# Opening stage: v of two head pairs made token-major, the last K blocks of each half accumulator by accumulator, one accumulator parked in SBUF

## The chip, the cores and the metric

The kernel runs on one core of a Trainium2 chip. The core has a matrix engine (PE, which multiplies a stationary 128x128 block with a moving block of up to 512 columns and writes to PSUM), a vector engine (DVE), a scalar engine (ACT), a general engine (POOL), and an engine whose queue issues DMAs (SP). SBUF is the working memory of 128 partitions; PSUM has eight banks of 512 float32 per partition. The metric is the time on the device in microseconds, of one launch; less is better.

## What is computed

One layer of a streaming encoder for 1024 tokens of width 1024. What bears on the change is its beginning:

```python
mod = (c_act @ w_ada[l] + b_ada[l])[:, None, :]
sh_m, sc_m, g_m, sh_f, sc_f, g_f = jnp.split(mod, 6, axis=-1)
h = rmsnorm(x, norm_mix_w[l]) * (1 + sc_m) + sh_m
z, xbc, dt_raw, q, k, v = jnp.split(h @ w_in[l], IN_SPLITS, axis=-1)
y_ssd = ssd_mixer(z, xbc, dt_raw, ...)
y_att = chunk_attention(q, k, v, rel_bias[l])
x = x + g_m * (jnp.concatenate([y_ssd, y_att], axis=-1) @ w_out[l])
...
```

The attention has 8 heads of 64 features, which the kernel handles as four pairs of 128 features. A query block of 64 tokens sees its own and the 8 blocks before it, with a bias by relative position. The rest (the mixer, the output projection, a gated feed-forward network with a causal convolution, the final norm) comes after it and isn't touched.

## The kernel before

**Numbers in two parts.** Products are made exact enough by splitting each float32 operand into a high and a low part of the type fp32r. `mm3` (lines 75 to 78) issues three matmuls for each product: high by high, high by low, low by high. `split` (lines 80 to 86) makes the two parts, the high one as a copy on ACT (line 85) and the low one as a difference on DVE (line 86); with a scale, these are lines 82 and 83.

**The opening stage** (lines 272 to 304) makes q, k and v of pairs 0 and 1. Tokens are handled in two halves of 512 (`hh`), the contraction over 1024 features in eight K blocks of 128 (`kt`). For a K block of half 0 it loads two columns of `w_ada` and reduces them on DVE (`mod_col`, line 134) to the scale `amix` and the shift `bmix`, loads the block's weights `w_first[kt]` and splits them into `wsh` and `wsl` or `wsl2` (read through `ws_lo`). Then, in both halves, four transposes on PE (line 290) turn the normalised token tiles `xts` into a PSUM tile `tps`; `h_block` (lines 241 to 244) applies scale and shift on ACT into `hf`, of which there is one buffer, and DVE writes the high and low parts hH and hL; and six accumulators in six PSUM banks (tag `acc0`) each get one `mm3` of 512 columns: q0, k0, v0, q1, k1, v1, with features in the partitions and tokens in the columns. Of the other two banks (tag `tp0`) the transposes use one each.

**Evacuation.** After the last K block of a half, `evac_qkv` (lines 217 to 236) is called for the six accumulators. q: two scaled splits of 64 partitions. k: two splits, and four DMAs that copy kh and kl to the other 64 partitions (line 228, issued by SP). v: a copy to SBUF on ACT (line 230), four transposes on PE (line 232), and a split into the tile `v`, which has tokens in its partitions, as the weighted sum of the attention needs it.

**Memory that is used again.** The q and k tiles and the eight tiles `xts` share twelve buffers (`qkp`): pair 1's kh and kl lie where token tiles 4 to 7 were, which half 1 still transposes. So k1 of half 0 can't be evacuated before half 1's transposes are done. When the opening stage ends, its pool `s0` (weights, `hf`, and so on) and its banks `ps0` are given back, and the attention's tiles (`pp` for softmax rows, `bp` for bias, `ptp`, and the PSUM pool `ps1` with the tags s, tp, acc and pv) take their place.

**The attention** (`attention`, line 403, with `attn_scores` and `attn_pv`) goes through four steps `u` of two token tiles each for a pair. Scores on PE (line 335), bias and row maximum on DVE (line 347), exponential on ACT (line 350), reciprocal on DVE (line 352), scaling on POOL (line 353), transposes on PE (lines 379, 382), the weighted sum on PE (lines 390, 391). Between scores and sums of some steps, functions given as `extra` are traced: for pairs 1 and 2 these are the GEMMs of q, k and v of the next pair (`gemm_part`, line 431; 512-column matmuls named acc<-hH,wh and so on in the profile). They still use the v path with transposes.

**Order.** A planner places the instructions of all engines by a simulated timeline, so the order on an engine isn't that of the program text: in the profile part of pair 2's GEMM already runs during pair 0's attention. Where `T.on` is set, `InOrder` (lines 45 to 61) chains each PE instruction behind the one traced before it. SP issues its DMAs in order, and one that waits holds back those behind it.

Of the kernel before, what the change touches and what calls it, by code (L numbers as in the profile page):

```python
# [10 lines left out]
F32 = mybir.dt.float32  # L11
# [5 lines left out]
P = 128  # L17
# [47 lines left out]
def tile_block(ctx: ExitStack, tc: tile.TileContext, x, crep, pk, w_ada, w_first, w_ft, w_z,  # L65
# [111 lines left out]
    qkp = es_at.enter_context(tc.tile_pool(name="qkp", bufs=12, side="right"))  # L177
    vp = es_at.enter_context(tc.tile_pool(name="vp", bufs=2, side="right"))
    es_0 = ExitStack()
# [31 lines left out]
    qk = {}  # L211

    def new_pair(p):
        qk[p] = {n: [qk_tile(F32R) for _ in range(2)] for n in ("q", "kh", "kl")}
        qk[p]["v"] = vp.tile([P, NT, 2, 2, 64], F32R, tag="v", name="v")

# [52 lines left out]
    for st in range(4):  # L269
        norm1(st)  # L270
    adw = wu.tile([P, 2, 1024], F32, tag="w2", bufs=1, name="adat2")
    for hh in range(2):
        accs = [ps0.tile([P, 512], F32, tag="acc0", bufs=6, name="acc0") for _ in range(6)]
        for kt in range(KT):
            if hh == 0:
# [7 lines left out]
                for st in range(4, NT):  # L283
                    if XL[st - 4] == kt:
                        V.tensor_copy(xts[st][:, 0:1], amix[:, kt:kt + 1])
                        nc.sync.dma_start(xts[st], x[st * P:(st + 1) * P, :])
                        norm1(st)
            tps = ps0.tile([P, 512], F32, tag="tp0", bufs=2, name="tp0")
            for j in range(4):
                T.transpose(tps[:, j * P:(j + 1) * P], xts[4 * hh + j][:, kt * P:(kt + 1) * P], ident)  # L290
            tmp = s0.tile([P, 512], F32, tag="hf", bufs=1, name="hf")
            hi, lo = ht(hh, kt)
            h_block(tps, amix, bmix, kt, hi, lo, tmp)
            for t in range(6):
                w = slice(t * P, (t + 1) * P)
                mm3(c4(accs[t]), wsh[:, kt, w], ws_lo(kt)[:, w], hi, lo,
                    kt == 0, kt == KT - 1)
        for t in range(6):
            tmp = tps = None
            if t % 3 == 2:  # L300
                tmp = s0.tile([P, 512], F32, tag="hf", bufs=1, name="hfv")
                tps = ps0.tile([P, 512], F32, tag="tp0", bufs=2, name="tpv")
            evac_qkv(t // 3, t % 3, hh, accs[t], tmp, tps)
    es_0.close()
# [4 lines left out]
    ptp = es_at.enter_context(tc.tile_pool(name="ptp", bufs=1, side="right", reuse_waits="tile"))  # L309
    es_p1 = ExitStack()  # L310
    ps1 = es_p1.enter_context(tc.tile_pool(name="ps1", bufs=1, space=PSUM, reuse_waits="tile"))
# [45 lines left out]
    def attn_pv(p, u, h, p0, p1):  # L357
# [7 lines left out]
        if lo0 < lo1:  # L365
            blocks.append((lo0, 0, 128))
        pv = ps1.tile([P, 512], F32, tag="pv", bufs=1, name="pv")[:, 0:256]
        nb = len(blocks)
# [62 lines left out]
    def gemm_part(p, which):  # L431
        if which == 0:
            new_pair(p)
        wh, wl = wu_pair(w_ft[8 + 3 * (p - 2) + which], A, G)
        outs = [ps1.tile([P, 512], F32, tag="acc", bufs=1, name="acc") for _ in range(2)]
        gemm_ft(wh, wl, outs)
        for hh in range(2):
            tmp = tps = None
            if which == 2:
                tmp, tps = p_tile()[:, 0:512], tp_tile()  # L440
            evac_qkv(p, which, hh, outs[hh], tmp, tps)
# [17 lines left out]
    part = lambda p, w: (lambda: gemm_part(p, w))  # L459
    attention(0)  # L460
    for p in (1, 2):
# [113 lines left out]
    def z_tile(ch, st, wz):  # L575
        if st % 4 < 2:
            ps = ps1.tile([P, 512], F32, tag=("acc", "pv")[st % 4], bufs=1, name="zps")[:, 0:260]
        else:
# [816 lines left out]
def _layout(i):  # L1395
# [12 lines left out]
    pairs = [w[:, p * P:(p + 1) * P] for p in range(4) for w in (wq, wk, wv)]  # L1408
    w_first = np.concatenate(pairs[0:6], axis=1).reshape(KT, P, 768)
    ft = [w_in[:, 512 + P * j:512 + P * (j + 1)] for j in range(8)] + pairs[6:]  # L1410
# [31 lines left out]
```

## Time and profile before

| what | value |
|---|---|
| median of 3 runs (lowest, highest) | 1228.65 us (1228.55, 1231.7) |
| the profiled execution: its time | 1230.44 us |
| the profiled execution: its span | 1228.7 us |
| mean granted PE clock | 0.984 |
| DMA, mean over the span | 123 GB/s |

The busy time of each engine in the stretches around the opening stage, from the view that sums it by stretches:

| stretch, us | what | PE busy | DVE busy | ACT busy | POOL busy | granted clock |
|---|---|---|---|---|---|---|
| 18 to 57 | half 0 | 38.21 | 36.63 | 18.19 | 9.37 | 1.00 |
| 57 to 64 | between the halves | 3.88 | 5.76 | 5.22 | 1.48 | 0.77 |
| 64 to 101 | half 1 | 36.52 | 11.01 | 9.30 | 0.00 | 0.95 |
| 101 to 106 | before the attention | 1.99 | 4.82 | 3.97 | 0.00 | 0.91 |
| 106 to 128 | attention, pair 0 | 20.88 | 13.64 | 13.46 | 14.73 | 0.87 |

How to read the profile lines that follow. A line of the timeline gives the start and the length in us, the engine, the line of the kernel, the operation, the tile written and the tiles read, the shape and the count of merged instructions; in brackets stands how long the engine stood idle before it, and what it waited for. PE is the matmul, PEld the load of the stationary operand, SPq the issue of a DMA. Matmuls are pipelined, so a line's length is longer than the distance to the next start; the distance is what a matmul costs in a stream. A line grouped by operation gives the count, the total busy time in us, the mean in ns, and the idle time ahead of the group with what ended it.

### The profile page before, as it was taken

Reading aid. Unit: us, or ns where it says so; the run is one execution under the profiler, and the core shown is the slowest. Engines: PE = TensorE matmul, PEld = TensorE weight load, DVE = VectorE, ACT = ScalarE, POOL = GpSimd, SP = SyncE. Lnnn points to the kernel's source line nnn. Section 1 sums busy time; section 2 is a strip of 40 time slices with the busy share of each in tenths; the row PEclk is TensorE's granted clock in tenths of the full one; section 3 lists DMA queues with packets and bytes.
Section 4 is the critical chain, followed back from the end, with each engine's and each line's share of the span. In section 5 each row is a group of like instructions: output and inputs, shape, how many; then the busy total and the mean of one; then the engine's idle time right before and its main releaser. Section 6 shows DMA issues by size and latency. Waiting matters only on the chain.

```text
span 1228.7 us, 15497 instructions
## 1 busy us (share of the span) xinstructions
PE 1169.9 (95%) x5722; PEld 978.2 (80%) x5722; DVE 945.2 (77%) x1419; ACT 590.0 (48%) x994; POOL 198.9 (16%) x174
## 2 busy tenths in 40 slices
PE   5898999989999989999899999999999999999995
PEld 3787788878878968888688888888888888888884
DVE  7835655589699678747799988988889869766976
ACT  4525656573333567666554433443334445433443
POOL 1303655474220034300000000000000000000002
PEclk9998999999999989999999999999999999999998
DMA  9712112134356301132122233222232277733533
GB/s 335 266 37 67 48 44 65 46 114 169 107 179 212 121 1 53 37 127 95 54 84 106 100 129 129 78 93 106 111 129 78 95 282 271 275 121 121 172 120 137
DMA packets 56395, 150.86 MB, mean 123 GB/s; under 512 B 5632, under 2 KB 5760, under 8 KB 54912
## 3 DMA queue, kind: packets, MB, share of 16 engines
q1 hardware_dynamic: 49264, 125.49, 29.9%
q10 hardware_dynamic: 7056, 24.38, 5.0%
q8 instruction: 45, 0.74, 0.2%
q14 instruction: 30, 0.25, 0.1%
HBM read 116.56 MB, written 29.10 MB: 119 GB/s over the span
## 4 chain that ended last, share of the span: by engine, by line
PE 68%; DVE 6%; ACT 1%; DMA 1%; issue 1%; POOL 0%; DVEq 0%; POOLq 0%; SPq 0%; ACTq 0%
PE wops L629 6%; PE dn L76 6%; PE dn L77 6%; PE dn L78 6%; PE uY L76 5%; PE uY L77 5%; PE uY L78 5%; PE uZ L76 3%; PE uZ L77 3%; PE uZ L78 3%; PE uX L77 3%; PE uX L76 3%; PE uX L78 3%; PE s L76 2%; PE s L77 2%; PE s L78 2%
## 5 line engine op out<-in xcount | busy, mean ns | idle before, releaser
L861 POOL TENSOR_TENSOR st<-st,mhalf 128x1 f32<-128x1 f32 x16 | 12.7, 799 | 691.8 <-DVE st L860 680.4
L76 PE MATMUL dn<-w 128*128 128x512 f32 x308 | 111.9, 389 | 0.0
L77 PE MATMUL dn<-w 128*128 128x512 f32 x308 | 111.9, 389 | 0.0
L78 PE MATMUL dn<-w 128*128 128x512 f32 x308 | 103.3, 389 | 0.0
L353 POOL TENSOR_SCALAR p<-p,st 128x640 f32<-128x640 f32 (+4 forms) x64 | 98.5, 1554 | 29.1 <-DVE st L352 27.2
L76 PE MATMUL uY<-tH,w 128*128 128x512 f32 x256 | 99.7, 389 | 1.8 <-ACT w L58 1.8
L77 PE MATMUL uY<-tL,w 128*128 128x512 f32 x256 | 99.6, 389 | 0.0
L78 PE MATMUL uY<-tH,w 128*128 128x512 f32 x256 | 99.6, 389 | 0.0
L629 PE MATMUL wops<-hH,yhl 128*128 128x512 f32 x224 | 76.3, 409 | 4.9 <-DVE yhl L86 2.1
L85 ACT ACTIVATE w<-ya 128x1024 fp32r<-128x1024 f32 (+1 forms) x41 | 39.1, 954 | 84.7 <-PE uY L78 82.7
L77 PEld LDWEIGHTS dn<-w 128*128 128x128 f32 x308 | 57.8, 188 | 12.1
L78 PEld LDWEIGHTS dn<-w 128*128 128x128 f32 x308 | 57.8, 188 | 12.0
L76 PEld LDWEIGHTS dn<-w 128*128 128x128 f32 x308 | 57.8, 188 | 11.9
L347 DVE CUSTOM_DVE_ANT_0 p<-s,bias 128x640 f32<-128x640 f32 (+4 forms) x64 | 40.7, 650 | 25.5 <-PE tp L379 8.7
L76 PEld LDWEIGHTS uY<-tH,w 128*128 128x128 f32 x256 | 48.0, 188 | 12.2 <-ACT w L58 2.2
L78 PEld LDWEIGHTS uY<-tH,w 128*128 128x128 f32 x256 | 48.0, 188 | 10.0
L77 PEld LDWEIGHTS uY<-tL,w 128*128 128x128 f32 x256 | 48.1, 188 | 9.9
L86 DVE TENSOR_TENSOR pt<-tp,pt 128x512 fp32r<-128x512 f32 (+2 forms) x72 | 41.8, 595 | 17.4 <-ACT pt L85 10.2
L85 ACT ACTIVATE pt<-tp 128x512 fp32r<-128x512 f32 (+2 forms) x72 | 36.4, 523 | 38.5 <-PE tp L379 17.9
L629 PEld LDWEIGHTS wops<-hH,yhl 128*128 128x128 f32 x224 | 43.1, 194 | 14.7 <-DVE yhl L86 2.5
L85 ACT ACTIVATE w<-xs 128x1024 fp32r<-128x1024 f32 (+1 forms) x41 | 38.9, 952 | 32.2 <-PE uY L78 32.2
L76 PE MATMUL s<-hH,wh 128*128 128x512 f32 x128 | 50.6, 395 | 1.0 <-DVE ct L450 1.0
(432 smaller groups left out, 3405.5 us busy)
## 6 DMA issues: line engine op xcount, KB each, us to landing
gz<-a ACTq DMA_DIRECT2D x10, 1024.0 KB, 5.3
wos<-in_w_ada_dram SPq DMA_DIRECT2D x18, 512.0 KB, 4.4
ya<-in_w_up_dram SPq DMA_DIRECT2D x11, 768.0 KB, 4.0
xs<-in_w_up_dram SPq DMA_DIRECT2D x11, 768.0 KB, 4.1
adat<-in_w_ada_dram SPq DMA_DIRECT2D x16, 512.0 KB, 5.6
raws<-in_w_ft_dram SPq DMA_DIRECT2D x14, 512.0 KB, 3.8
qk<-in_w_ada_dram SPq DMA_DIRECT2D x14, 512.0 KB, 4.4
gy<-a ACTq DMA_DIRECT2D x10, 512.0 KB, 2.6
```

The source lines that it names most:

```text
L76: T.matmul(ps, lh, rh, start=start, stop=False, skip_group_check=more)
L77: T.matmul(ps, lh, rl, start=False, stop=False, skip_group_check=more)
L78: T.matmul(ps, ll, rh, start=False, stop=stop, skip_group_check=more)
L85: i = A.activation(hi, src, AF.Copy) if ehi is A else ehi.tensor_copy(hi, src)
L86: return i, elo.tensor_tensor(lo, src, f32(hi), ALU.subtract)
L347: V.tensor_tensor_reduce(out=dst, in0=src, in1=bsl, scale=-1.0, scalar=3e38, op0=ALU.add, op1=ALU.min, accum_out=nm)
L353: G.tensor_scalar(pv_, pv_, rr, None, op0=ALU.mult)
L629: i = op(*a, **k)
L861: G.tensor_tensor(r, ms, mhalf[:, 0:1], ALU.pow)
```

## The change

The first six column blocks of the weights are put in a new order: q0, k0, q1, k1, v0, v1. v of both pairs is then computed with the token block of h as the stationary operand and the 256 columns of v0 and v1 as the moving one (`first_v`), so that tokens come out in the partitions. Its PSUM tiles `vps` hold two token blocks by 256 columns each and use the tags acc and pv of a pool `psv`, which the attention goes on to use. `evac_v` splits from PSUM straight into one tile `vv` for all pairs (pair p uses part p % 2).

Only four accumulators remain (`acc0` and `acc1`, two banks each). Up to `split_at` (K block 6 in half 0, K block 4 in half 1) the K blocks run one after the other as before. The remaining ones run accumulator by accumulator, with PE's order chained: in half 0 first v, then q0, k0, q1, k1, each evacuated when it is done, except k1, which ACT copies to `k1` in SBUF; in half 1 q0, k0, q1, k1, each evacuated, then the parked `k1`. The remaining K blocks of v of half 1 and their evacuation are traced within step 0 of pair 0's attention. `hf` gets a second buffer.

```diff
@@ -175,7 +175,9 @@
     yp = es_y.enter_context(tc.tile_pool(name="yp", bufs=1, side="right"))
     es_at = ExitStack()
     qkp = es_at.enter_context(tc.tile_pool(name="qkp", bufs=12, side="right"))
-    vp = es_at.enter_context(tc.tile_pool(name="vp", bufs=2, side="right"))
+    vp = es_at.enter_context(tc.tile_pool(name="vp", bufs=1, side="right"))
+    es_p1 = ExitStack()
+    psv = es_p1.enter_context(tc.tile_pool(name="psv", bufs=1, space=PSUM, reuse_waits="tile"))
     es_0 = ExitStack()
     s0 = es_0.enter_context(tc.tile_pool(name="s0", bufs=1, side="right"))
     ps0 = es_0.enter_context(tc.tile_pool(name="ps0", bufs=1, space=PSUM))
@@ -210,9 +212,11 @@
 
     qk = {}
 
+    vv = vp.tile([P, NT, 2, 2, 2, 64], F32R, name="v")
+
     def new_pair(p):
         qk[p] = {n: [qk_tile(F32R) for _ in range(2)] for n in ("q", "kh", "kl")}
-        qk[p]["v"] = vp.tile([P, NT, 2, 2, 64], F32R, tag="v", name="v")
+        qk[p]["v"] = vv[:, :, p % 2]
 
     def evac_qkv(p, which, hh, ps, tmp, tps):
         d = qk[p]
@@ -269,8 +273,37 @@
     for st in range(4):
         norm1(st)
     adw = wu.tile([P, 2, 1024], F32, tag="w2", bufs=1, name="adat2")
+
+    def first_qk(acc, n, hh, kts):
+        w = slice(n * P, (n + 1) * P)
+        for kt in kts:
+            mm3(c4(acc), wsh[:, kt, w], ws_lo(kt)[:, w], *ht(hh, kt), kt == 0, kt == KT - 1)
+
+    def first_v(vps, hh, kts):
+
+        for b, ps in enumerate(vps):
+            for kt in kts:
+                h = T.on
+                T.on, T.last = True, T.last if h else None
+                for j in range(2):
+                    mm3(ps[:, j], hth[hh][:, 2 * b + j, kt, :], htl[hh][:, 2 * b + j, kt, :],
+                        wsh[:, kt, 512:768], ws_lo(kt)[:, 512:768], kt == 0 and j == 0, kt == KT - 1, True)
+                T.on = h
+
+    def evac_v(vps, hh):
+        for b, ps in enumerate(vps):
+            st = 4 * hh + 2 * b
+            o = vv[:, st:st + 2].rearrange("p j q h s d -> p (j q h) s d")
+            split(o[:, :, 0, :], o[:, :, 1, :], ps.rearrange("p j (a d) -> p (j a) d", d=64), A, V)
+
     for hh in range(2):
-        accs = [ps0.tile([P, 512], F32, tag="acc0", bufs=6, name="acc0") for _ in range(6)]
+        accs = [ps0.tile([P, 512], F32, tag="acc0", bufs=2, name="acc0") for _ in range(2)]
+        if hh == 0:
+            tp_ = [ps0.tile([P, 512], F32, tag="tp0", bufs=2, name="tp0")]
+        accs += [ps0.tile([P, 512], F32, tag="acc1", bufs=2, name="acc1") for _ in range(2)]
+        vps = [psv.tile([P, 2, 256], F32, tag=t, bufs=1, name="vps") for t in ("acc", "pv")]
+        split_at = KT - (2, 4)[hh]
+        tail = range(split_at, KT)
         for kt in range(KT):
             if hh == 0:
                 mod_col(SC_M + kt, wu.tile([P, 1024], F32, tag="wh", name="adat"))
@@ -285,29 +318,38 @@
                         V.tensor_copy(xts[st][:, 0:1], amix[:, kt:kt + 1])
                         nc.sync.dma_start(xts[st], x[st * P:(st + 1) * P, :])
                         norm1(st)
-            tps = ps0.tile([P, 512], F32, tag="tp0", bufs=2, name="tp0")
+            tps = tp_.pop() if tp_ else ps0.tile([P, 512], F32, tag="tp0", bufs=2, name="tp0")
             for j in range(4):
                 T.transpose(tps[:, j * P:(j + 1) * P], xts[4 * hh + j][:, kt * P:(kt + 1) * P], ident)
-            tmp = s0.tile([P, 512], F32, tag="hf", bufs=1, name="hf")
+            tmp = s0.tile([P, 512], F32, tag="hf", bufs=2, name="hf")
             hi, lo = ht(hh, kt)
             h_block(tps, amix, bmix, kt, hi, lo, tmp)
-            for t in range(6):
-                w = slice(t * P, (t + 1) * P)
-                mm3(c4(accs[t]), wsh[:, kt, w], ws_lo(kt)[:, w], hi, lo,
-                    kt == 0, kt == KT - 1)
-        for t in range(6):
-            tmp = tps = None
-            if t % 3 == 2:
-                tmp = s0.tile([P, 512], F32, tag="hf", bufs=1, name="hfv")
-                tps = ps0.tile([P, 512], F32, tag="tp0", bufs=2, name="tpv")
-            evac_qkv(t // 3, t % 3, hh, accs[t], tmp, tps)
+            if kt < split_at:
+                for n in range(4):
+                    first_qk(accs[n], n, hh, (kt,))
+                first_v(vps, hh, (kt,))
+        T.on, T.last = True, None
+        if hh == 0:
+            first_v(vps, 0, tail)
+            evac_v(vps, 0)
+            for n in range(4):
+                first_qk(accs[n], n, 0, tail)
+                if n < 3:
+                    evac_qkv(n // 2, n % 2, 0, accs[n], None, None)
+            k1 = s0.tile([P, 512], F32, name="k1")
+            A.activation(k1, accs[3], AF.Copy)
+        else:
+            for n in range(4):
+                first_qk(accs[n], n, 1, tail)
+                evac_qkv(n // 2, n % 2, 1, accs[n], None, None)
+            evac_qkv(1, 1, 0, k1, None, None)
+        T.on = False
     es_0.close()
 
 
     pp = es_at.enter_context(tc.tile_pool(name="pp", bufs=8, side="right", reuse_waits="tile"))
     bp = es_at.enter_context(tc.tile_pool(name="bp", bufs=3, side="right", reuse_waits="tile"))
     ptp = es_at.enter_context(tc.tile_pool(name="ptp", bufs=1, side="right", reuse_waits="tile"))
-    es_p1 = ExitStack()
     ps1 = es_p1.enter_context(tc.tile_pool(name="ps1", bufs=1, space=PSUM, reuse_waits="tile"))
     ya = yp.tile([P, NT, 512], F32, tag="y", name="ya")
     pt = ptp.tile([P, 6, 512], F32R, name="pt")
@@ -364,7 +406,7 @@
         blocks.append((i1, 128, 128))
         if lo0 < lo1:
             blocks.append((lo0, 0, 128))
-        pv = ps1.tile([P, 512], F32, tag="pv", bufs=1, name="pv")[:, 0:256]
+        pv = psv.tile([P, 512], F32, tag="pv", bufs=1, name="pv")[:, 0:256]
         nb = len(blocks)
         done = 0
         while done < nb:
@@ -432,7 +474,7 @@
         if which == 0:
             new_pair(p)
         wh, wl = wu_pair(w_ft[8 + 3 * (p - 2) + which], A, G)
-        outs = [ps1.tile([P, 512], F32, tag="acc", bufs=1, name="acc") for _ in range(2)]
+        outs = [psv.tile([P, 512], F32, tag="acc", bufs=1, name="acc") for _ in range(2)]
         gemm_ft(wh, wl, outs)
         for hh in range(2):
             tmp = tps = None
@@ -457,7 +499,7 @@
         return last.ins
 
     part = lambda p, w: (lambda: gemm_part(p, w))
-    attention(0)
+    attention(0, {0: (lambda: first_v(vps, 1, tail), lambda: evac_v(vps, 1))})
     for p in (1, 2):
         attention(p, {u: [part(p + 1, w) for w in ws] for u, ws in GP.items()})
         for w in GPL:
@@ -574,7 +616,7 @@
 
     def z_tile(ch, st, wz):
         if st % 4 < 2:
-            ps = ps1.tile([P, 512], F32, tag=("acc", "pv")[st % 4], bufs=1, name="zps")[:, 0:260]
+            ps = psv.tile([P, 512], F32, tag=("acc", "pv")[st % 4], bufs=1, name="zps")[:, 0:260]
         else:
             ps = s_tile()[:, 0:260]
         for kt in range(KT):
@@ -1406,7 +1448,7 @@
         axis=1)
     wq, wk, wv = (w_in[:, 1544 + 512 * j:1544 + 512 * (j + 1)] for j in range(3))
     pairs = [w[:, p * P:(p + 1) * P] for p in range(4) for w in (wq, wk, wv)]
-    w_first = np.concatenate(pairs[0:6], axis=1).reshape(KT, P, 768)
+    w_first = np.concatenate([pairs[j] for j in (0, 1, 3, 4, 2, 5)], axis=1).reshape(KT, P, 768)
     ft = [w_in[:, 512 + P * j:512 + P * (j + 1)] for j in range(8)] + pairs[6:]
     w_ft = np.stack([w.reshape(KT, P, P).transpose(1, 0, 2).reshape(P, KT * P) for w in ft])
     wz = np.concatenate([w_in[:, 0:512], w_in[:, 1536:1544]], axis=1)
```

## The prediction, made before the changed kernel was run

> **What bounds the kernel now.** I read the page's first part, the chain of waits, then PE's timeline through the opening stage, then the busy time by stretches.
>
> ```profile
> PE 1169.9 (95%) x5722; PEld 978.2 (80%) x5722; DVE 945.2 (77%) x1419; ACT 590.0 (48%) x994; POOL 198.9 (16%) x174
> PE 68%; DVE 6%; ACT 1%; DMA 1%; issue 1%; POOL 0%; DVEq 0%; POOLq 0%; SPq 0%; ACTq 0%
> ```
>
> PE is the engine that is full and the one the last chain runs through. So what counts is where PE is not multiplying at full rate. In the opening stage that happens at two seams: after the last K block of half 0, and after the last K block of half 1.
>
> ```profile
> 56.53 0.40 PE L78 MATMUL acc<-hH,wsl 128*128 128x512 f32 x1
> 56.77 0.60 PE L232 MATMUL tpv<-ident,hfv 128*128 128x128 f32 x4
> 59.23 0.66 PE L232 MATMUL tpv<-ident,hfv 128*128 128x128 f32 x4 [1.86 <-ACT hfv L230]
> 59.72 0.62 PE L290 MATMUL tp<-ident,qk 128*128 128x128 f32 x4
> 61.61 1.97 PE L290 MATMUL tp<-ident,qk 128*128 128x128 f32 x8 [1.26 <-ACT hf L242]
> 63.23 2.48 PE L76 MATMUL acc<-hH,wsh 128*128 128x512 f32 x5
> 65.51 0.63 PE L77 MATMUL acc<-hL,wsh 128*128 128x512 f32 x1
> 67.22 0.56 PE L77 MATMUL acc<-hL,wsh 128*128 128x512 f32 x1
> ...
> 99.75 0.39 PE L76 MATMUL acc<-hH,wsh 128*128 128x512 f32 x1
> 100.89 0.40 PE L78 MATMUL acc<-hH,wsl 128*128 128x512 f32 x1
> 101.12 0.60 PE L232 MATMUL tpv<-ident,hfv 128*128 128x128 f32 x4
> 103.40 0.66 PE L232 MATMUL tpv<-ident,hfv 128*128 128x128 f32 x4 [1.68 <-ACT hfv L230]
> 103.81 0.42 PE L335 MATMUL s<-qk 128*128 128x128 f32 x2
> 105.56 0.66 PE L335 MATMUL s<-qk 128*128 128x128 f32 x2 [1.33 <-issue]
> 106.02 0.73 PE L76 MATMUL acc<-hH,wh 128*128 128x512 f32 x1
> 111.67 0.52 PE L77 MATMUL acc<-hL,wh 128*128 128x512 f32 x1
> ```
>
> The unit first. From 99.75 to 100.89 lie five starts: 1.14 / 5 = 0.228 us for one 512-column matmul at full rate. From 65.51 to 67.22 lie four: 0.43 us, about half rate.
>
> Seam 1: the last accumulation ends at 56.53 + 0.23 = 56.76 and the next begins at 63.23, 6.47 us later. Inside are 8 transposes of v (L232) and 12 of x (L290); the 12 are needed anyway, at about 0.11 us each 1.3 us. Lost: 5.15 us. Then, from 63.23 to 67.22, nine starts take 3.99 us instead of 2.05: another 1.94.
>
> Seam 2: 101.12 to 106.02 is 4.90 us, of it four 128-column score matmuls (0.24 us) are needed. Lost: 4.66. From 106.02 to 111.67 thirteen starts take 5.65 us instead of 2.96: 2.69. Both seams together lose 14.4 us.
>
> **The change part by part.** *v token-major.* It removes 16 transposes (inside the seams, counted there), the four copies on ACT ahead of them, and PE's waits on those copies. 96 matmuls of 512 columns become 192 of 256. The trace has nearly this shape in the z stage, with new weights for every matmul (the copy's row stands first):
>
> ```profile
> L230 ACT ACTIVATE hfv<-acc 128x512 f32<-128x512 f32 x4 | 2.4, 592 | 0.3 <-PE acc L78 0.2
> ...
> 399.36 0.28 PE L76 MATMUL zps<-wzh,hH 128*128 128x260 f32 x1
> 400.92 0.28 PE L77 MATMUL zps<-wzl,hH 128*128 128x260 f32 x1
> L77 PEld LDWEIGHTS zps<-wzl,hH x64: 187/188/193, 380.5 to 425.8; 128*128 128x128 f32 x64
> ```
>
> Thirteen starts in 1.56 us: 0.120 us at 260 columns, so 0.118 at 256. 192 x 0.118 - 96 x 0.228 = 22.7 - 21.9 = +0.8 us. A load is listed with 188 ns, yet the pitch is 0.120, so loads overlap each other here.
>
> *The end of half 0.* The six first K blocks run as now. Then comes a PE order written by hand: v of blocks 6 and 7, then q0, k0, q1, k1, each with its own two blocks. The second group of v already needs block 7, which now comes last.
>
> ```profile
> 48.60 1.52 PE L76 MATMUL acc<-hH,wsh 128*128 128x512 f32 x6
> 49.40 0.95 DVE L86 TENSOR_TENSOR wsl<-raws,wsh 128x768 fp32r<-128x768 f32 x1
> 50.72 0.69 DVE L244 TENSOR_TENSOR hL<-hf,hH 128x512 fp32r<-128x512 f32 x1
> 53.37 2.88 DVE L267 TENSOR_SCALAR qk<-qk,st 128x1024 f32<-128x1024 f32 x1 [0.75 <-POOL st L117]
> L83 DVE SCALAR_TENSOR_TENSOR qk<-acc,qk 64x512 fp32r<-64x512 f32 x12 | 8.3, 689 | 9.1 <-ACT qk L82 8.8
> ```
>
> hL of block 7 is ready at 50.72 + 0.69 = 51.41; PE, which reaches block 6 at 48.60, will stand before it for about 1 us. Queued behind in the hand-written order are q0 to k1, which nothing may pass. The second hf buffer could bring hL forward at most to where wsl is ready (50.35), a gain of 1; DVE is in order and full there, so I take 0. From 51.41 remain 16 v matmuls (1.9 us) and 24 of 512 columns (5.5 us): half 0 ends at 58.8, 2.0 later than now. In exchange v, q0 and k0 are evacuated meanwhile (each two steps on ACT and two on DVE, about 0.59 and 0.69 us by the rows of L230 and L83). The first h block of half 1 needs the last normalised x tile (53.37 + 2.88 = 56.25), then transposes, ACT and DVE, with some four evacuation steps ahead of it on DVE: about 60. So half 1 starts multiplying at about 60.4, bounds 58.8 (everything hidden) and 63.2 (as now). I take the half rate there as gone, since this gap is a third of the shorter one that it followed. Parking k1 adds one ACT copy of about 0.59 us, hidden in the same stretch; its four evacuation steps and four k copies stay late, since its targets are the buffers of x tiles 4 to 7, which half 1 still transposes.
>
> *Half 1.* 96 x 0.228 + 96 x 0.118 = 33.2 us, plus 24 transposes not yet done, 2.6: the matmuls end at 96.2. The last 5.7 us of these (48 of 256 columns) are v's tail, now traced inside the first attention step. q0, k0, q1, k1 and the parked k1 are evacuated under the tail. The v tail holds banks "acc" and "pv"; acc's part is evacuated (0.59 + 0.69 us) under pv's 24 matmuls. So the GEMM of pair 2 can begin at about 96.5 at full rate, against 106.02 + 2.69: PE is 12.2 us ahead.
>
> *The wait it adds.* The bias tiles and the softmax tiles lie where s0 lay, and v's tail still reads s0's weights. So the bias load can't be issued before v's tail ends; SP issues it in order behind the k copies.
>
> ```profile
> 105.66 0.47 SPq L228 DMA_DIRECT2D qk<-qk  x1
> 105.03 0.54 SPq L408 DMA_DIRECT2D bias<-in_bias_dram  x1
> 108.69 0.14 POOL L409 MEMSET bias<- 64x64 f32 x1 [50.21 <-DMA bias<-in_bias_dram]
> 108.86 0.29 DVE L347 CUSTOM_DVE_ANT_0 p<-s,bias 128x128 f32<-128x128 f32 x1 [2.68 <-POOL bias L409]
> 113.84 0.42 DVE L347 CUSTOM_DVE_ANT_0 p<-s,bias 128x256 f32<-128x256 f32 x1 [1.15 <-PE s L335]
> 115.25 18.66 POOL L353 TENSOR_SCALAR p<-p,st 128x256 f32<-128x256 f32 x12 [1.75 <-DVE st L352]
> 126.60 0.69 DVE L83 SCALAR_TENSOR_TENSOR qk<-acc,qk 64x512 fp32r<-64x512 f32 x1
> ```
>
> Issue to first softmax step: 108.86 - 105.03 = 3.83 us. With the issue between 96.5 and 98.1 (the last k copies ahead of it, about 0.5 us each) I take 97.0; softmax starts at 100.8, 8.0 us earlier. Does PE's 12.2 count, or this 8.0? The first attention pair is paced by POOL, back to back from 115.25 for 18.66 us, and the GEMM of pair 2 stops after its first half until 126.60, when the q tiles it writes become free. So the lower end is nearer. The 1.15 us wait for a score matmul that ran behind half-rate ones should mostly go: I take 8.5.
>
> *After that* the same instructions follow. The busy time by stretches (first column after the length is PE):
>
> ```profile
> 130.00:290.00 160.00, 151.76 (x883) 129.04 (x884) 99.71 (x266) 90.68 (x211) 98.10 (x69) 0.99 0.24 79
> 290.00:330.00 40.00, 40.00 (x216) 34.36 (x215) 29.56 (x40) 15.72 (x26) 8.28 (x5) 1.00 0.26 85
> ```
>
> PE is 95% busy, then wholly, so the shift should be carried to the end. **Sum:** on the profiled execution 1228.7 - 8.5 = 1220.2 us of span (1230.44 as its own time); the median shown is 1228.65, equal to the span, so 1220.2.
>
> **A rule on the half rate.** "TensorE: Matmul & The Clock Gate" of the Trainium skill (part 1) says that the array falls to half rate after an idle window of some 3.4 us and recovers after a busy one of that length; part 4 adds that transposes don't count as busy in the same way. The trace agrees: gaps of 6.5 and 4.9 us, each with little but transposes, were followed by 4.0 and 5.7 us at 0.43 us pitch. By this rule a seam of 1.6 us stays at full rate, as in the sum; but it gives a rival, below.
>
> **The rivals.** (1) *Half rate comes back in the first attention pair.* PE's 24 GEMM matmuls are used up 5.5 us after 96.5, at 102, while scores and transposes come in numbers only from about 105 (113.84 less 8.5). Price: one stretch like the second, 2.7 us; or seam 1 opens until 63.2: 2.8. Together with the forecast that is 1222.9 or 1223.0; with the half rate of seam 1 besides (1.9), 1224.9. For it: the 18.66 us of POOL; against: POOL then hides part of it.
>
> (2) *PE's whole lead counts*: 12.2 us, 1216.5. Against: the POOL row.
>
> (3) *Given back later.* The order of all engines in the attention stage is planned anew. PE lacks 8.2 us of the 160 from 130 to 290; an order with twice these holes gives 1228.4. Nothing in the rows asks for it; nothing excludes it.
>
> (4) *Slower: one v tile for all pairs.* If writing v of pair 2 (or 3) counts as touching the tile that pair 1 (or 2) reads, every later weighted sum of that pair waits for a whole v GEMM, 48 x 0.228 = 10.9 us, at two places: up to 21.9, 1242. It decides from 4.3 us at each. Against it:
>
> ```profile
> 22.74 0.42 DVE L243 CAST hH<-hf 128x512 fp32r<-128x512 f32 x1
> 24.89 0.39 PE L78 MATMUL acc<-hH,wsl 128*128 128x512 f32 x1
> 187.54 0.69 DVE L86 TENSOR_TENSOR v<-tp,v 128x512 fp32r<-128x512 f32 x1 [0.46 <-ACT v L85]
> 192.51 0.33 PE L390 MATMUL pv<-pt,v 128*128 128x256 f32 x1
> ```
>
> DVE writes block 1 of hH at 22.74 while PE reads block 0, interleaved in one tile, until 24.89; and v of pair 2 is complete at 188.2, ahead of the sums from 192.51 on, so at most those before it could be held up.
>
> **How the numbers follow.** Forecast (gain 6.5 to 11): 0.55. Rival 1 (gain 3.7 to 6.5): 0.14. Rival 2: 0.08. Rival 3: 0.15. Rival 4: 0.08. A measurement of this kernel tells about 0.3% (3.7 us) from no change: faster 0.76, same 0.15, slower 0.09. The range 1213.5 to 1228.5 takes in both bounds of the sum (6.9 to 12.2, and the 14.4 of both seams) and half of rival 3.
>
> **What would show it.** In the changed profile: no L232-like transposes before the first attention step; 256-column matmuls at 0.118 us; half 0 ending near 58.8 after a short wait on hL; half 1 starting near 60.4 without 0.43 us pitches; matmuls of half 1 done near 96; first softmax step near 100.8; then the same distance of about 8.5 us up to the end. Wrong would be a first softmax step after 105, a new hole in the attention pairs, or sums of pair 1 or 2 waiting for a v evacuation.

## The result, and the profile after

| | before | after |
|---|---|---|
| median (lowest, highest), 5 runs each | 1228.85 us (1228.55, 1231.7) | 1234.94 us (1233.96, 1236.51) |
| the profiled execution: time, span | 1230.44 us, 1228.7 us | 1236.51 us, 1234.8 us |

The changed kernel is slower by 6.1 us: the ratio is 1.0052, with a 95% interval from 1.0037 to 1.0066. The prediction said 1220.2 us with a range from 1213.5 to 1228.5, so sign and range were both wrong.

First the busy times from the page of the changed kernel:

```profile
PE 1169.8 (95%) x5802; PEld 983.1 (80%) x5802; DVE 944.7 (77%) x1419; ACT 589.0 (48%) x991; POOL 199.9 (16%) x174
```

PE's busy time is that of before to 0.1 us (1169.9 there). So the 6.1 us are not work. They are time in which PE stood still, and the question is where. Following the same events through both traces tells it (us from the start of each span; the columns on the right are experiments of the next section):

| event | predicted | before | after | e1 | e4 | e11 |
|---|---|---|---|---|---|---|
| half 1 starts multiplying | 60.4 | 63.23 | 63.41 | 62.93 | 60.39 | 60.74 |
| GEMM of pair 2 starts | 96.5 | 106.02 | 102.12 | 101.31 | 97.48 | 97.83 |
| first bias load issued | 97.0 | 105.03 | 105.49 | 104.69 | 100.86 | 97.39 |
| first softmax step | 100.8 | 108.86 | 109.72 | 109.25 | 105.26 | 103.87 |
| GEMM of pair 2 goes on | | 130.69 | 129.32 | 128.62 | 124.53 | 123.03 |
| last weighted sum taken over | | 328.5 | 328.6 | 326.4 | 322.2 | 321.8 |
| first state-space matmul (ydp) | | 433.1 | 440.2 | 431.5 | 427.4 | 426.3 |
| span | | 1228.7 | 1234.8 | 1226.9 | 1222.7 | 1222.1 |

Two separate things are in the third and fourth columns. Up to the last sum of the attention at 328.5 the change has gained nothing: the opening stage did not bring what was forecast. And between 328 and 440, in a part that the diff touches only in the pool of two tiles, 7 us are lost. The loss is the whole result, so it comes first.

**The loss at 433 to 440.** The busy time by stretches has it (length, then PE, PEld, DVE, ACT, POOL, granted clock, share of the DMA engines, GB/s). Before:

```profile
400.00:450.00 50.00, 47.56 (x345) 44.55 (x344) 35.16 (x67) 30.59 (x75) 9.25 (x8) 0.97 0.22 75
```

After:

```profile
400.00:450.00 50.00, 43.52 (x314) 41.57 (x313) 34.00 (x65) 27.55 (x67) 8.57 (x8) 0.90 0.23 75
```

PE is busy 4.0 us less, and the clock is lower. PE's timeline there, before:

```profile
432.97 0.28 PE L78 MATMUL s<-wzh,hL 128*128 128x260 f32 x1
433.09 1.89 PE L629 MATMUL ydp<-xdt,th 128*128 128x64 f32 x16
...
437.41 0.71 PE L629 MATMUL xps<-ct,bt 128*128 128x128 f32 x4 [1.05 <-DVE zs L587]
...
439.74 0.79 PE L629 MATMUL wops<-hH,yhl 128*128 128x512 f32 x1 [1.39 <-DVE zs L587]
```

DVE's, before:

```profile
439.27 0.41 DVE L587 SCALAR_TENSOR_TENSOR zs<-zt,s 128x260 f32<-128x260 f32 x1
```

After (L671 is the line of the same helper, L629 that of the same DVE step):

```profile
433.39 0.28 PE L78 MATMUL s<-wzh,hL 128*128 128x260 f32 x1
440.15 3.67 PE L671 MATMUL ydp<-xdt,th 128*128 128x64 f32 x16 [6.48 <-DVE zs L629]
```

and DVE's, after:

```profile
439.68 0.41 DVE L629 SCALAR_TENSOR_TENSOR zs<-zt,s 128x260 f32<-128x260 f32 x1
```

Before, the state-space matmul ydp follows the last z matmul at once. After, it stands 6.48 us until DVE has read the last z tile. It can't be the data: before, these 16 matmuls ran from 433.09 on, while DVE's last zs step came only at 439.27. What is left is the place that ydp writes: PSUM. And then it runs at half rate, 3.67 us for the 1.89 of before: by the records of the granted clock a stretch at half rate begins inside the wait, at 436.4 us, and lasts until 446.6.

The diff explains how the place can have changed. Tiles of a PSUM pool get banks in the order in which pools are opened. Before, one pool `ps1` held all of s (four banks), tp (two), acc and pv, so s lay at the bottom. After, `psv` with acc and pv is opened ahead of it and takes the two lowest banks, and s moves up by two, into banks 2 to 5. The pool from which the state-space stage takes ydp is opened at the other end and gets banks 4 to 7. So in the changed kernel it takes half of s; and the z tiles that are finished last are those in s (`z_tile`: the first two of each four go to acc and pv, the other two to s). By the same reading the kernel before had a milder form of this wait: its tiles xps and wops come from the low end, where s lay, and the lines above have them waiting 1.05 and 1.39 us for the same zs steps. This was a reading of the code, and e1 and e2 test it.

**The gain that didn't come.** The opening stage, after, PE:

```profile
51.49 0.38 PE L58 MATMUL vps<-wsh,hH 128*128 128x256 f32 x1 [0.45 <-DVE hH L247]
...
52.21 0.38 PE L58 MATMUL vps<-wsh,hL 128*128 128x256 f32 x1 [0.22 <-DVE hL L248]
...
59.69 0.60 PE L323 MATMUL tp<-ident,qk 128*128 128x128 f32 x4
62.95 0.66 PE L323 MATMUL tp<-ident,qk 128*128 128x128 f32 x4 [2.66 <-ACT hf L246]
63.41 0.96 PE L76 MATMUL acc<-hH,wsh 128*128 128x512 f32 x3
```

The transposes of v are gone, and yet half 1 starts at 63.41, no earlier than before, because PE waits 2.66 us for `hf`, the scaled h block that ACT makes. DVE, ACT and POOL in the same stretch:

```profile
54.12 2.88 DVE L271 TENSOR_SCALAR qk<-qk,st 128x1024 f32<-128x1024 f32 x1 [0.75 <-POOL st L117]
56.92 1.27 DVE L86 TENSOR_TENSOR v<-vps,v 128x512 fp32r<-128x512 f32 x2
...
59.58 0.69 DVE L83 SCALAR_TENSOR_TENSOR qk<-acc,qk 64x512 fp32r<-64x512 f32 x1 [0.66 <-ACT qk L82]
```

```profile
58.95 0.59 ACT L82 ACTIVATE qk<-acc 64x512 fp32r<-64x512 f32 x1 [2.51 <-DVE qk L83]
...
61.02 0.59 ACT L85 ACTIVATE qk<-acc 64x512 fp32r<-64x512 f32 x1 [0.86 <-DVE qk L86]
61.63 0.60 ACT L340 ACTIVATE k<-acc 128x512 f32<-128x512 f32 x1
62.13 1.44 ACT L246 ACTIVATE hf<-tp,bmix,amix 128x512 f32<-128x512 f32 x2
```

```profile
54.05 2.40 POOL L86 TENSOR_TENSOR wl<-raws,wh 128x1024 fp32r<-128x1024 f32 x1
56.41 2.85 POOL L86 TENSOR_TENSOR wl<-raws,wh 128x1024 fp32r<-128x1024 f32 x1
```

Read them backwards. `hf` is made at 62.13, last in ACT's queue, behind evacuation steps of q0 and k0 and the copy that parks k1 (L340). The steps of q0 and k0 stood 2.51 us waiting for DVE. DVE came late to them because the normalisation of the last token tile took 2.88 us; the rows of its seven fellows have 0.75 us. It was released at 54.12, just after POOL began the first of two subtractions, and it ends at 57.00, 0.55 us after that one.

Further on, after, PE, SP, DVE and POOL:

```profile
101.34 0.28 PE L58 MATMUL vps<-wsh,hL 128*128 128x256 f32 x1
102.12 0.50 PE L76 MATMUL acc<-hH,wh 128*128 128x512 f32 x1 [0.49 <-DVE v L86]
...
129.32 0.80 PE L76 MATMUL acc<-hH,wh 128*128 128x512 f32 x1 [0.33 <-DVE qk L83]
129.92 0.63 PE L77 MATMUL acc<-hL,wh 128*128 128x512 f32 x1
130.34 0.63 PE L78 MATMUL acc<-hH,wl 128*128 128x512 f32 x1
```

```profile
95.29 10.12 SPq L232 DMA_DIRECT2D qk<-qk  x11
105.49 22.80 SPq L450 DMA_DIRECT2D bias<-in_bias_dram  x5
```

```profile
93.92 0.69 DVE L83 SCALAR_TENSOR_TENSOR qk<-acc,qk 64x512 fp32r<-64x512 f32 x1 [0.66 <-ACT qk L82]
...
103.54 0.69 DVE L86 TENSOR_TENSOR qk<-acc,qk 64x512 fp32r<-64x512 f32 x1
109.72 0.29 DVE L389 CUSTOM_DVE_ANT_0 p<-s,bias 128x128 f32<-128x128 f32 x1 [5.49 <-POOL bias L451]
```

```profile
112.05 19.10 POOL L395 TENSOR_SCALAR p<-p,st 128x128 f32<-128x128 f32 x13
```

PE is through with v's tail at 101.5 and starts the GEMM of pair 2 at full rate at 102.12: it is 3.9 us ahead at that point, and the half rate of before is saved as well. But the bias load leaves SP only at 105.49, behind the k copies, which wait for the evacuation of k; its last DVE step ends at 104.2. So the softmax starts at 109.72, 0.9 us later than before. PE's lead is used up by waiting for it: the GEMM goes on at 129.32, 1.4 us earlier than before, and at half rate (0.42 us from 129.92 to 130.34).

### The profile page after: what moved, and what is told of

Same layout as the page of the kernel before. It is cut to its first block, busy times and chain, and to the rows that moved or that the text cites. A ratio compares the mean times of both kernels' runs of the same rounds, so it can differ in the third digit from the quotient of the medians.

```text
span 1234.8 us, 15648 instructions
## 1 busy us (share of the span) xinstructions
PE 1169.8 (95%) x5802; PEld 983.1 (80%) x5802; DVE 944.7 (77%) x1419; ACT 589.0 (48%) x991; POOL 199.9 (16%) x174
## 4 chain that ended last, share of the span: by engine, by line
PE 80%; DVE 11%; ACT 3%; DMA 2%; issue 2%; POOL 1%; SPq 0%; DVEq 0%; POOLq 0%; ACTq 0%
PE wops L671 6%; PE dn L77 6%; PE dn L76 6%; PE dn L78 6%; PE uY L76 5%; PE uY L78 5%; PE uY L77 5%; PE uZ L78 3%; PE uZ L76 3%; PE uZ L77 3%; PE uX L76 3%; PE uX L78 3%; PE uX L77 3%; PE acc L76 2%; PE acc L77 2%; PE acc L78 2%
## 5 line engine op out<-in xcount | busy, mean ns | idle before, releaser
L671 PE MATMUL wops<-hH,yhl 128*128 128x512 f32 x224 | 74.8, 402 | 3.5 <-DVE yhl L86 2.1
L671 PEld LDWEIGHTS wops<-hH,yhl 128*128 128x128 f32 x224 | 42.4, 190 | 12.9 <-DVE yhl L86 2.5
L1054 DVE SCALAR_TENSOR_TENSOR a<-cv,pkt,a 128x1023 f32<-128x1023 f32 (+1 forms) x40 | 51.2, 1279 | 0.1
```

What stands on the lines that cost most here:

```text
L671: i = op(*a, **k)
L1054: V.scalar_tensor_tensor(a[:, j:S], c[:, 0:S - j], w[2 - j], a[:, j:S], op0=ALU.mult, op1=ALU.add)
```

## The experiments

Theory A: the loss is the bank layout, and nothing else. Its rival B: the opening stage and the new order of the instructions cost the time, and the wait at 440 only passes it on. For the missing gain, C: the 2.88 us normalisation step holds up DVE, through it ACT, and so `hf`. E: the bias load is held up behind SP's k copies. D, which the expectations of e6 and e7 call F: whatever is won is lost again in the attention of pair 0. G: POOL's scaling sets the pace of pair 0; its rival H is DVE or the chain of one tile. T: accumulator by accumulator is itself what costs; the expectation of e5 counts the opposite, that it covers the evacuation, as part of C.

Runs of the kernel before beside e1, e2, e4 and e6: median 1229.57 us; beside e5, e7, e8 and e9: 1228.94 us; beside e10 and e11: 1229.4 us.

**e1: the changed kernel with the old layout.** `psv` is taken from the other end, so s returns to banks 0 to 3.

```diff
-    psv = es_p1.enter_context(tc.tile_pool(name="psv", bufs=1, space=PSUM, reuse_waits="tile"))
+    psv = es_p1.enter_context(tc.tile_pool(name="psv", bufs=1, space=PSUM, side="right", reuse_waits="tile"))
```

> The changed kernel with one edit: the pool psv (banks acc and pv) is opened on the other side of PSUM, so that the score tiles lie in banks 0 to 3 again, as in the kernel before. The order of instructions on every engine is the same as in the changed kernel. Theory A (banks): the first state-space matmul lost 6.5 us (433.1 before, 440.2 after) because its bank is now one of those that the last z tiles still hold; here it starts at about 433.5 again, the wait on the last z tile's evacuation (6.48 us) is gone, and the time is 1228 to 1229.5, about that of the kernel before. Theory B (order): the hole comes from the order in which the last z tiles are evacuated; then it stays and the time stays at 1234 to 1236.

Measured: 1228.55 us (1226.68 to 1230.0), ratio to before 0.9993, interval 0.9983 to 1.0003. PE's timeline of e1 at the place of the wait:

```profile
431.40 0.28 PE L78 MATMUL s<-wzh,hL 128*128 128x260 f32 x1
431.52 1.89 PE L671 MATMUL ydp<-xdt,th 128*128 128x64 f32 x16
```

The wait is gone, and so are the 6 us. Up to there the order of the instructions is the same as in the changed kernel on every engine, and the opening stage is the changed one, so B has no part in the 6 us.

**e2: the kernel before with the new layout.** Only a pool `psv` for acc and pv, opened ahead of `ps1`; the opening stage is that of before, and so is the order on every engine up to the place of the wait.

```diff
-    es_p1 = ExitStack()
+    es_p1 = ExitStack(); psv = es_p1.enter_context(tc.tile_pool(name="psv", bufs=1, space=PSUM, reuse_waits="tile")); [psv.tile([P, 512], F32, tag=t, bufs=1, name=t) for t in ("acc", "pv")]
...
-        pv = ps1.tile([P, 512], F32, tag="pv", bufs=1, name="pv")[:, 0:256]
+        pv = psv.tile([P, 512], F32, tag="pv", bufs=1, name="pv")[:, 0:256]
...
```

> The kernel before with one edit: acc and pv are taken from a pool opened ahead of ps1, so that PSUM is laid out as in the changed kernel in the attention and z stages; the opening stage is untouched and the order of instructions is that of the kernel before. Theory A (banks): the first state-space matmul waits for the last z tile, 6 to 7 us, and the time is 1234.5 to 1236. Theory B (order): nothing changes, 1228 to 1230.

Measured: 1234.45 us (1233.94 to 1235.94), ratio 1.0044, interval 1.0029 to 1.0059. PE's timeline of e2:

```profile
434.21 0.28 PE L78 MATMUL s<-wzh,hL 128*128 128x260 f32 x1
440.98 3.68 PE L629 MATMUL ydp<-xdt,th 128*128 128x64 f32 x16 [6.48 <-DVE zs L587]
```

The same wait of 6.48 us in a kernel without any other part of the change. Taking the layout away removes the loss, and adding it alone brings it (4.9 us here, 6.1 in the changed kernel, with intervals that overlap): A is shown.

**e4: e1, with the last token tile normalised by ACT.**

```diff
-        V.tensor_scalar(xts[st], xts[st], r, None, op0=ALU.mult)
+        A.activation(xts[st], xts[st], AF.Copy, scale=r) if st == NT - 1 else V.tensor_scalar(xts[st], xts[st], r, None, op0=ALU.mult)
```

> e1 with one edit: the last token tile of half 1 is normalised on ACT (about 1.06 us) instead of on DVE, where it took 2.88 us beside a POOL instruction of 5.2 us. Theory C: this stall pushed the evacuation of v, q0, k0 and with it hf of half 1's first K block back; half 1 then starts multiplying near 61.5 instead of 63.4, without the half-rate stretch (about 1.7 us), and v's tail ends 2 to 4 us earlier than 101.5. At the end of the run: if the opening's time counts, 2 to 4 us less than e1; if the first softmax step is tied to the k copies and those to the last accumulator's end, which moves too, the same 2 to 4. Rival D: the gain dies in the first attention pair, which POOL paces and where PE has nothing to fill with: within 1 us of e1.

Measured: 1226.53 us (1224.1 to 1228.35), ratio 0.9978, interval 0.9968 to 0.9989. The lines of e4, ACT, then PE:

```profile
52.83 1.16 ACT L271 ACTIVATE qk<-qk,st 128x1024 f32<-128x1024 f32 x1 [0.41 <-POOL st L117]
```

```profile
59.92 0.66 PE L323 MATMUL tp<-ident,qk 128*128 128x128 f32 x4 [0.92 <-ACT hf L246]
60.39 0.72 PE L76 MATMUL acc<-hH,wsh 128*128 128x512 f32 x2
```

The step now takes 1.16 us, the wait for `hf` falls from 2.67 in e1 to 0.92, and half 1 starts at 60.39. That this is the 60.4 of the prediction is luck, since the prediction's sum had the 2.88 us in it. With it the half rate after this seam is gone (the first stretch of half the granted clock begins at 105.9), the bias load goes out 3.8 us earlier than in e1 and the softmax starts 4.0 us earlier. C is shown for the seam, with one reservation: the planner also moved k0's second evacuation step behind `hf` (in e4 ACT makes `hf` at 59.10 and that step at 60.57), so how much of the 2.5 us is the stall's alone stays open. Of these 4.0 us the medians of e1 and e4 have 2.0 at the end, so D is not refuted: part of what was won is lost on the way.

**e9: the same edit in the kernel before.**

> The kernel before (opening stage untouched) with e4's edit alone: the last token tile normalised on ACT. Theory C says that the stall of DVE delays the first h block of half 1; in the kernel before, that block also waits for the evacuation of six accumulators (ACT and DVE busy from 54.9 to 63), which the edit doesn't shorten: half 1 starts within 1 us of 63.2 and the time stays within 1.5 us of the kernel before. Rival: the stall alone made the seam; then half 1 starts 2 to 3 us earlier without a half-rate stretch, and the time is 3 to 4 us less.

Measured: 1229.3 us (1226.18 to 1230.68), ratio 0.9994, interval 0.9981 to 1.0006. Half 1 starts at 62.91, 0.3 us earlier than before. There v's copies and transposes keep the seam open (PE still waits 1.55 us for `hfv` and 1.26 us for `hf`), so the stall costs nothing. So, as far as these runs can tell, the edit pays only with the changed opening, and the changed opening only with the edit: e1 can't be told from before, e9 can't, and e4, which has both, can.

**e5: e1 without the accumulator-by-accumulator part**, `split_at = KT` in both halves; all K blocks run one after the other.

```diff
-        split_at = KT - (2, 4)[hh]
+        split_at = KT - (0, 0)[hh]
```

> e1 (banks back) with split_at at 8 in both halves: all eight K blocks run one after the other, so the accumulators finish together and are evacuated after the last block, and nothing of v is left for the attention step; v stays token-major, k1 stays parked. If running the last blocks accumulator by accumulator is what covers the evacuation (theory C), the seams open again: half 1 starts 1 to 2 us later than in e1, the first softmax step some 2 to 4 us later than 109.2, and the time is 2 to 4 us more than e1 if a lead is carried to the end. If the lead dies in pair 0 anyway (rival D), within 1 us of e1.

Measured: 1228.4 us (1226.6 to 1230.77), ratio 0.9999, interval 0.9988 to 1.0011, against 0.9993 for e1. Half 1 starts at 61.19, earlier than in e1 (62.93), and the GEMM of pair 2 at 100.24 (101.31), but at half rate up to 106.3, and the softmax starts at 109.16 (109.25). So the hand-written order of the last K blocks neither costs nor brings anything that can be told, while the stall of DVE is in place. T falls, and so does the part's gain. Whether it brings something once the stall is mended wasn't tried.

**e6: e1, with the two bias loads of pair 0 on ACT's queue.**

```diff
-            nc.sync.dma_start(t, bias[2 * p + h])
+            (nc.scalar if p == 0 else nc.sync).dma_start(t, bias[2 * p + h])
```

> e1 with one edit: the two bias loads of pair 0 are issued from ACT's queue instead of SP's. Theory E: in the changed kernel they were ready when v's tail ended (101.5) but stood behind the last k copies until 105.5; here they are issued near 102, the first softmax step is at about 106 instead of 109.7, and if the lead is carried the time is 3 to 4 us less than e1. Rival F: the lead is lost again in the attention pairs (half-rate stretches, or PE without filler): within 1 us of e1.

Measured: 1229.09 us (1227.18 to 1231.37), ratio 1.0001, interval 0.9992 to 1.001. The loads left at 100.31 and the softmax started at 106.80, but POOL's timeline of e6 shows what came next:

```profile
111.10 0.15 POOL L451 MEMSET bias<- 64x64 f32 x1 [4.50 <-DMA bias<-in_bias_dram]
...
111.54 5.63 POOL L395 TENSOR_SCALAR p<-p,st 128x128 f32<-128x128 f32 x6
```

The memset of the third bias tile, whose load was still on SP, stands in POOL's queue ahead of the scaling. The experiment told nothing of E, since it moved the wait by one tile instead of taking it away.

**e7: e4, with three bias loads on ACT's queue.**

```diff
+            (nc.scalar if 2 * p + h < 3 else nc.sync).dma_start(t, bias[2 * p + h])
```

> e4 with the first three bias loads (both of pair 0 and the first of pair 1) issued from ACT's queue. In e6 only pair 0's two were moved: the third stayed on SP's queue until 105.0, landed late, and POOL, which clears corners of that tile ahead of the first scalings, stood 4.5 us before it, so e6 did not test its theory. ACT issues them after its last evacuation step, near 99 against 100.9 in e4; first softmax step near 103.3 instead of 105.3, POOL's scalings from about 105.6 instead of 107.6. Theory E: the lead is carried, 1.5 to 2.5 us less than e4. Rival F: it is lost in pair 0, within 0.7 us of e4.

Measured: 1223.06 us (1221.53 to 1225.51), ratio 0.9948, interval 0.9932 to 0.9964. Faster than every kernel so far, but its profile was not ahead of that of e4 (spans 1223.8 and 1222.7), and the two ratios come from different comparisons. Hence e10 and e11 below.

**e8: e4, with the second head's scaling of pair 0 on ACT.**

```diff
-            G.tensor_scalar(pv_, pv_, rr, None, op0=ALU.mult)
+            A.activation(pv_, pv_, AF.Copy, scale=rr) if p == 0 and h == 1 else G.tensor_scalar(pv_, pv_, rr, None, op0=ALU.mult)
```

> e4 with one edit: for pair 0 the scaling of the second head's softmax rows is done on ACT instead of POOL (8 of 16 scalings). Theory G (POOL paces pair 0, and PE can't fill since the GEMM of pair 2 has to wait for pair 0's last scores): POOL's 19.1 us run shrinks to 10 to 12, pair 0's last scores and the second half of the GEMM of pair 2 (124.5 in e4) come 3 to 6 us earlier, and the time is 2 to 5 us less than e4. Rival H (DVE or the latency of one tile's chain paces pair 0): the GEMM resumes within 1 us of 124.5, the time is that of e4 within 1 us, or more if ACT becomes the bound.

Measured: 1225.02 us (1224.21 to 1226.14), ratio 0.9963, interval 0.9948 to 0.9978, which overlaps that of e4. POOL now has gaps of up to 2.49 us, but the GEMM goes on at 127.17, later than the 124.53 of e4. POOL's and PE's timelines of e8:

```profile
113.33 1.56 POOL L395 TENSOR_SCALAR p<-p,st 128x512 f32<-128x512 f32 x1 [2.49 <-DVE st L394]
```

```profile
127.17 0.78 PE L76 MATMUL acc<-hH,wh 128*128 128x512 f32 x1
```

The busy time from 104 to 130 us (columns as above), e4, then e8:

```profile
104.00:130.00 26.00, 21.11 (x113) 17.23 (x113) 17.19 (x59) 16.79 (x43) 23.70 (x24) 0.93 0.15 54
104.00:130.00 26.00, 20.23 (x99) 16.97 (x100) 18.45 (x60) 21.68 (x52) 13.21 (x18) 0.80 0.15 50
```

So relieving POOL alone doesn't bring the GEMM forward. But the edit also raised ACT's busy time from 16.79 to 21.68 us, and the granted clock was lower, so it isn't shown what sets the pace of pair 0 in its place, and G is weakened, not refuted.

**e10 and e11: e4 and e7 again, side by side.**

> The kernel of e4_norm7_act again, beside e11, so that the two share the same runs of the kernel before. If the two times measured earlier (1226.53 and 1223.06, ratios 0.9978 and 0.9948 from different comparisons) are a real difference, this one gives a ratio of about 0.998 and e11 one 0.003 lower. If the difference came from the runs they were compared with, the two give ratios within 0.001 of each other, somewhere from 0.995 to 0.998.

> The kernel of e7_bias3_actq again (the first three bias loads on ACT's queue, besides the normalise step on ACT). Theory that the bias path counts: ratio 0.995, below e10's interval, about 3 us less time than e10. Rival, that the first softmax step 1.4 us earlier is lost again in pair 0 (the profile of e7 shows the GEMM of pair 2 resumed at 125.56, 1.0 later than in e4): the same ratio as e10 within 0.001.

Measured: e10 1226.88 us (1225.04 to 1227.84), ratio 0.9976, interval 0.9966 to 0.9986; e11 1223.8 us (1221.6 to 1224.37), ratio 0.9953, interval 0.9939 to 0.9966. Against the same runs of before, e11 is 3.1 us faster than e10. DVE and PE in e11:

```profile
103.87 0.29 DVE L389 CUSTOM_DVE_ANT_0 p<-s,bias 128x128 f32<-128x128 f32 x1 [3.92 <-PE s L377]
```

```profile
123.03 0.80 PE L76 MATMUL acc<-hH,wh 128*128 128x512 f32 x1 [0.19 <-DVE qk L83]
```

The bias load leaves at 97.39, close to the 97.0 of the prediction. The first softmax step now waits for PE's scores, not for the bias. E is borne out as a second cause, with the first out of the way. The planner also put the first steps of pair 0's attention and a few instructions near 625 us in another order, so the 3.1 us belong to the edit with this order, not surely to the earlier load alone. Which of the microseconds after 104 make up the 3.1 is not settled: the start of the softmax is 1.4 us earlier than in e4 and 1.5 than in e10, and the last weighted sum, at 321.8, is 0.3 earlier than in e4 but 3.0 than in e10 (324.8), though these two are one kernel. The rest may be the half rate, whose stretches vary from execution to execution (last section). e11 is 5.6 us below before and 11.1 below the changed kernel as it was given.

## Why the prediction was wrong

**The step that failed** is "After that the same instructions follow". It carried the shift to the end on the ground that PE is nearly full. From the z stage on the instructions are indeed the same and in the same order on PE; but the diff moves acc and pv into a pool opened earlier, and the prediction costed that line at nothing. It moved the four banks of s, and 330 us further on a stage had to wait 6.48 us for a bank that it now shared with s. With the 0.4 us by which the last z matmul was already later, that put ydp back by 7.1 us. Half rate then cost 1.8 us more at ydp, while the waits of xps and wops fell away; 6.1 us were left at the end. The prediction's rival "given back later" had the right place in time, after the opening, but another mechanism, a new order with holes in the attention. PE's order did change a little in the last pair's attention, but the last sum comes at 328.6 as before, and e1 has that order without the loss. Without this loss the forecast would have failed too: e1 is 1.0 us below before, within an interval that takes in no change, where 8.5 were forecast. The steps that lost the gain follow.

**The end of half 0** was about right: 59.69 instead of 58.8, with waits of 0.45 and 0.22 us where about 1 was expected.

**The start of half 1**, forecast at 60.4, came at 63.41, just outside the bound given as "as now". The prediction quoted the normalisation's 2.88 us and added it up to 56.25, but then counted only four DVE steps ahead of the h block; there are six, v's two with them. It left out that q0's and k0's steps alternate between ACT and DVE, one after the other, and that `hf` is queued behind them on ACT. The copy that parks k1, which it had as hidden, stands right before `hf` too (61.63). With the 2.88 us on DVE replaced by 1.16 on ACT, half 1 starts 2.5 us earlier (e4 against e1, where the planner's order changed a little too).

**The half rate after it** was taken as gone. It stayed, from 64.4 to 67.8 by the granted clock, because the seam stayed open; in e4, where the seam is shorter, it is gone, and none of the five profiles with that edit and the changed opening (e4, e7, e8, e10, e11) has a half-rate stretch before 105. So the condition was right, and it wasn't met.

**v token-major** costs what was said: from 99.91 to 101.34 us there are twelve 256-column starts, 0.119 us each, against 0.118.

**The bias load**, forecast at 97.0, left at 105.49. The prediction knew that SP's k copies stand ahead of it and gave them about 0.5 us each. It didn't ask when they can start: the last k step of the evacuation ends at 104.2, because the steps on ACT and DVE run as a relay (DVE waits 0.66 to 0.68 us for ACT before each step from 93.92 to 99.36), and the two v steps come between the last ones. With the load on another queue (e11) it leaves at 97.39.

**The gain of 8.5 us** assumed the softmax at 100.8. Even e11 has it at 103.87: in the changed order PE computes 24 GEMM matmuls from 97.83 on ahead of the first scores at 103.41, where before four score matmuls stood ahead of the GEMM at 106.02. The 3.83 us from issue to softmax were taken over from an order that the change undid.

**The lower end of the two leads counts**: the reasoning that PE's lead is worth nothing beyond the softmax's was right. In the changed kernel PE was 3.9 us ahead and the softmax 0.9 behind, and at 328.6 nothing was left. **One v tile for all pairs** cost nothing: v of pair 2 is written at 184.4 us, as before (184.3).

## What to carry to other kernels

When a diff opens a pool earlier or splits one, write down which banks or addresses every later tile gets, and look for stages that now share one: a line that computes nothing cost 6 us at a place 330 us away, and PE's busy time, equal in both, already says that the loss is a wait. When a stall is taken away, follow each queue that the next step stands in (here ACT's, then SP's), since the seam closes only when the last of them is free: e4's step alone brought nothing on the kernel before. And carry a lead forward only as far as the next wait for something that didn't get earlier.

## What the runs showed of the hardware

**A normalisation step on DVE took 2.88 us where POOL's subtraction had begun just before it, and 0.75 us elsewhere**, in the kernel before as in the changed one, for the same 128x1024 float32 shape. By the rows shown, DVE's step is released 0.07 us after POOL's first subtraction starts and ends 0.55 us after it ends (56.45); that subtraction takes 2.40 us, which is also the median of all 14 of its kind, and POOL's second one takes 2.85 us, 0.45 more. That is one waiting for the other, not both running more slowly. The Trainium skill's "SBUF: two separate sides" in "SBUF — State Buffer" says so: VectorE's two-port operations and GpSimd share a pair of ports, and who has it keeps it for a whole instruction. The trace agrees. The same step on ACT took 1.16 us next to the same POOL work.

**The half rate comes and goes in steps of 3.41 us on one grid per execution.** The starts of the half-rate stretches in the records of the granted clock, in us from the start of the span (without the last one, in the final 11 us), and their distances in units of 3.413 us:

```
after  64.4   112.2  129.2  248.7  436.4  463.7  603.7
steps  0      14.0   19.0   54.0   109.0  117.0  158.0
e4     105.9  242.4  433.5  450.6  590.5
steps  0      40.0   96.0   101.0  142.0
```

The Trainium skill's "TensorE: Matmul & The Clock Gate" (part 1) describes a free-running window of that length; the grid agrees. What was not expected is its effect on timing. e4 and e10 are one kernel, but counted from the start of the span their grids lie 0.04 and 2.65 us past a whole step, and e10's execution has a stretch at 125.5 us that e4's lacks. So it seems that where the grid lies, and not the kernel alone, decides whether a gap costs half rate; two executions don't prove it. Runs of e9 lie between 1226.18 us, at a mean granted clock of 0.990, and 1230.68 us, at 0.984. So single executions of one kernel lie up to 4.5 us apart, the slower one at the lower granted clock, and the span of one profile isn't enough to rank kernels that are 3 us apart.
